# A two-layer decoder trunk on one core: attention scores two tiles apart, output projection by two blocks, weights of the tokens ahead of the first gather, expert output combined two weight tiles later

## The chip, the cores and the metric

The kernel runs on one core of one Trainium2 chip. The metric is device time in microseconds of one launch; three executions of the kernel before give its median. A separate profiled execution gives the trace. In it a busy TensorE is called PE, its weight loads PEld, VectorE DVE, ScalarE ACT, SyncE (which issues the weight loads) SP. Every time below is counted from the start of the profiled span.

## The reference

There are 256 tokens of width 1024 and two layers. Each layer adds a mixer of three branches and a feed-forward part; the second layer's feed-forward part has eight experts, of which each token uses two.

```python
for l in range(2):
    h = rms_norm(x, norm_mix[l]);  p = h @ w_in[l]          # split into xa, ba, ca, q, k, v, xc, gc, gates
    y_a = (ba * conv3(ca * xa)) @ wo_a[l]
    y_b = attention(q, k, v) @ wo_b[l]                       # 8 heads of 64, q and k normed and rotated, causal
    y_c = (gelu(gc) * rg_lru(conv4(xc))) @ wo_c[l]
    x = x + (sig(gA) * y_a + sig(gB) * y_b + sig(gC) * y_c) @ w_o[l]
    h = rms_norm(x, norm_ffn[l])
    x = x + (swiglu(h) if l == 0 else moe_swiglu(h))

def moe_swiglu(t, router, w_gate, w_up, w_down):             # 8 experts of width 3584
    top_v, top_i = top_k(t @ router, 2)
    comb = sum(one_hot(top_i, 8) * softmax(top_v)[..., None], axis=1)
    for e in range(8):
        out = out + comb[:, e, None] * (silu(t @ w_gate[e]) * (t @ w_up[e])) @ w_down[e]
```

## The kernel before

All weights are float32 and are read once, in loads of 1 MiB that SP issues. A load holds two weight tiles of 1024 columns. Each tile is split into a high part `whi`, an ACT copy (L175), and a low part `wlo`, a DVE subtraction (L176), and PE multiplies three times: high by high, high by low, low by high. Activations are split in the same way (`xn`, `xg`, `mo`, `x_e`, `y`; L194 on ACT and L195 on DVE). A tile is 24 matmuls of 256 columns in the dense stages (L184, L185, L187) and 6 of 512 columns in the expert stage (L972 gate and up, L1018 down).

`Flow` sets the order. `step` splits the tile that is two ahead, then issues the matmuls of the current tile, then runs what was put off with `flow.soon` (it runs after the matmuls of the next tile), and then takes entries from a queue, `rate` of them for each tile. `flow.push` appends to that queue. `flow.flush(n)` runs n of its entries at once. Where PE (or PE, DVE and ACT) is under a manual schedule, the instructions stand as they are issued; elsewhere a scheduler may move them.

**Scores.** `mixer` pushes the scores of head pairs 0 and 1 one after the other. A pair is eight small matmuls into two PSUM banks of the kind "at" (L596 and L598); DVE reads them with mask and maximum (L605), ACT takes exponentials (L609, which loads its table first) and scales them (L613).

**Output projection.** `mix_out` multiplies the merged branches `mo` by `w_o`. Before, a weight tile holds one block of 128 outputs over all eight k tiles, so the first tile already wants all eight parts of `mo`. In layer 0 two blocks share a bank and one addition of 128x512 takes both (`ev_o`); in layer 1 each block has its own (`ev_1`). After each pair of blocks `after` runs the next norm's part: `Moe.pair` in layer 1, with the router's sums `ps_l`, the squares `ps_v` and the transposed tokens `ps_tr`.

**Route.** `Moe.route` takes the root of the squares' sums on ACT (`rt`), selects two experts for each token on DVE (`sel`), counts places with two matmuls (`ps_r`) and builds a selection matrix `oh`. `start` gathers the tokens of the first two experts in eight groups (32 matmuls `ps_x`, split by L194 and L195 into `x_e`), and only then come the gate tiles; `weigh` (reciprocals, softmax of two, a count `ps_n`) and `slots` (`ps_rs`) are taken from the queue among them.

**Experts.** `rest` runs eight experts by seven chunks; a chunk is four gate tiles, four up tiles and four down tiles, the down tiles of a chunk beside the next chunk. In an expert's last chunk `ps_y` is complete after the second down tile for its first half and after the fourth for the second half. `split_act` then makes `y` from it, and `combine` (`ps_cb`, four matmuls, L1039, and two additions to `acc`, L1042) is put off with one `flow.soon`, so it stands after the next tile.

Of the kernel before, what the change touches and what calls it, by code (L numbers as in the profile page):

```python
# [17 lines left out]
P = 128  # L18
D = 1024
KT = 8  # L20
# [44 lines left out]
def trunk(ctx, tc, xt, cst, par, rgw, w_in, w_br, w_o, f_gu, f_d, m_g, m_u, m_d, out):  # L65
# [294 lines left out]
    def mixer(l, norm, br, mp):  # L360
# [324 lines left out]
        flow.push(hs[0][0], hs[1][0])  # L685
# [20 lines left out]
    def mix_out(l, ms, after, end=True):  # L706
        for hf in range(2):
            def ev_o(j, ps, hf=hf):
                q = 4 * hf + 2 * j
                dve.tensor_tensor(x2(q), x2(q), ps, OP.add)  # L710
                after(q // 2)

# [5 lines left out]
            blocks(w_o[l, hf], KT, ms, ev_o if end else ev_1, single=not end)  # L718
# [54 lines left out]
    class Moe:  # L773
# [9 lines left out]
        def pair(self, j):  # L783

            if j == 0:

                self.x = self.tile([P, 2, 3, KT, P], "x_e", FR)
                self.acc = self.tile([P, 2, D], "acc")
                self.h2h, self.h2l = two([P, 2, D], "h2")
                self.ps_l = [bank("sm", 3, "ps_l") for _ in range(2)]  # L790
                self.ps_v = [bank(t, b, "ps_v") for t, b in (("sm", 3), ("at", 2))]
# [10 lines left out]
            act.activation(sq, x2(2 * j), AF.Square)  # L802

# [6 lines left out]

            def squares():
                for t in range(2):
                    for k in (2 * j, 2 * j + 1):
                        pe.matmul(self.ps_v[t][:, 0:1], sq[:, k % 2, t * P:t * P + P], ones[:, 0:1], start=k == 0, stop=k == KT - 1)
# [16 lines left out]
            flow.soon(sums, squares, turn)  # L831
# [5 lines left out]

        def route(self):
            T = self.tile
            lg, self.rt = self.lg, T([P, 2], "rt")  # L840
            for t in range(2):
                act.activation(self.rt[:, t:t + 1], self.ps_v[t][:, 0:1], AF.Sqrt, bias=eps_t, scale=1.0 / D)
# [3 lines left out]
            sq, sel = small.tile([P, 2, S], F32, tag="sq", bufs=2, name="gt"), T([P, 2, 8], "sel", FR)  # L846
            gt, eq = (sq[:, i, 0:128].rearrange("p (t a b) -> p t a b", t=2, a=8) for i in range(2))
# [16 lines left out]
            self.sel = sel.bitcast(F32)  # L864

        def weigh(self):
# [4 lines left out]
            ps_n, cmax = bank("sm", 2, "ps_n"), T([P, 1], "cmax")  # L871
            pe.matmul(ps_n[:, 0:8], ones, sel[:, 0], start=True, stop=False)
            pe.matmul(ps_n[:, 0:8], ones, sel[:, 1], start=False, stop=True)
# [244 lines left out]
    with tc.tile_pool(name="psB", bufs=1, space=PSUM) as ps:  # L1118
        psums.append(ps)
        start()  # L1120
        with tc.manual_schedule(engines={PE, DVE, ACT}):
            rest()
# [100 lines left out]
```

## Time and profile before

| what | value |
|---|---|
| median of three runs | 1670.65 us (1670.14, 1670.65, 1673.53) |
| profiled execution | 1673.91 us |
| its span, first to last instruction | 1672.4 us |
| mean granted clock of PE | 0.993 |
| busy: PE, DVE, ACT | 98%, 81%, 70% |
| MB moved by DMA, mean rate | 472.03 MB, 282 GB/s |

A granted clock of 1.00 is 2.4 GHz and 0.50 is 1.2 GHz. The share of busy time is a mean over stages with different limits, and the expert stage, from about 678 us to the end, is over half of the span. In a timeline row the columns are start, duration, engine, line, operation and tiles, and in brackets how long the engine sat idle before it and for whom; matmuls overlap, so the pace of a row of matmuls is read from their starts. A row with "x4" holds four instructions that follow each other.

### The profile page before, as it was taken

The page shows a single profiled execution, that of the slowest core. Times are in us where ns is not written, and L with a number is a line of the kernel's source. Part 1 is how long each engine was busy: PE and PEld are TensorE (multiplying, and loading weights), DVE is VectorE, ACT ScalarE, POOL GpSimd, SP SyncE. Part 2 cuts the span into 40 slices and gives each one's busy share as a digit, 9 for nine tenths or more (in the row PEclk, how much of TensorE's full clock was granted, in tenths as well). Part 3 has the DMA queues.
Part 4 walks back from the last instruction along what each step waited for, and adds up shares of the span by engine and source line. Part 5 has one row for each costly group of instructions (what it writes and reads, how often), then busy time and mean ns, then how long its engine had stood idle before and what let it go on. Part 6 is the DMA issues. An engine that isn't in the chain of part 4 may idle for free.

```text
span 1672.4 us, 25362 instructions
## 1 busy us (share of the span) xinstructions
PE 1637.2 (98%) x9786; PEld 1439.9 (86%) x9786; DVE 1358.3 (81%) x1582; ACT 1178.4 (70%) x1443; POOL 0.7 (0%) x9
## 2 busy tenths in 40 slices
PE   6999999999999999999999999999999999999998
PEld 6989999999998999788888888888888888888886
DVE  7667777555676775889998999998999998999987
ACT  6577556444557755787777787777778777778775
POOL 0000000000000000000000000000000000000000
PEclk9999999999999999999999999999999999999999
DMA  8544555546653457799999999999999999999980
GB/s 322 184 150 152 198 181 182 197 142 222 227 178 128 158 199 308 298 370 364 354 362 346 353 365 376 343 367 332 352 365 368 353 362 339 339 377 370 347 335 27
DMA packets 67232, 472.03 MB, mean 282 GB/s; under 512 B 7456, under 2 KB 7584, under 8 KB 11040
## 3 DMA queue, kind: packets, MB, share of 16 engines
q1 hardware_dynamic: 66960, 470.19, 76.1%
q8 instruction: 78, 1.28, 0.3%
q14 instruction: 50, 0.41, 0.1%
q10 hardware_dynamic: 144, 0.16, 0.0%
HBM read 469.27 MB, written 1.05 MB: 281 GB/s over the span
## 4 chain that ended last, share of the span: by engine, by line
PE 91%; DVE 6%; issue 1%; ACT 1%; DMA 0%; SPq 0%; DVEq 0%; ACTq 0%
PE ps_gu L972 35%; PE ps_y L1018 16%; PE ps_mm L184 9%; PE ps_mm L187 9%; PE ps_mm L185 9%; DVE wlo L176 3%; PE ps_qk L478 3%; PE ps_tt L995 1%; PE ps_v L478 1%; PE ps_d L185 1%; PE ps_d L184 1%; PE ps_d L187 1%; PE ps_x L914 1%; DVE y L195 1%; DVE acc L1042 1%
## 5 line engine op out<-in xcount | busy, mean ns | idle before, releaser
L176 DVE TENSOR_TENSOR wlo<-raw,whi 128x1024 fp32r<-128x1024 f32 (+1 forms) x796 | 945.8, 1218 | 171.3 <-ACT whi L175 153.0
L175 ACT CAST whi<-raw 128x1024 fp32r<-128x1024 f32 (+1 forms) x796 | 824.1, 1051 | 328.8 <-PE ps_mm L185 138.9
L972 PE MATMUL ps_gu<-whi,x_e 128*128 128x512 f32 x1792 | 487.4, 394 | 0.0
L972 PEld LDWEIGHTS ps_gu<-whi,x_e 128*128 128x128 f32 x1792 | 330.8, 188 | 66.1
L972 PE MATMUL ps_gu<-wlo,x_e 128*128 128x512 f32 x896 | 276.4, 390 | 0.0
L1018 PE MATMUL ps_y<-whi,t 128*128 128x512 f32 x896 | 240.3, 390 | 0.0
L184 PE MATMUL ps_mm<-xn,whi 128*128 128x256 f32 x864 | 207.6, 282 | 0.0
L185 PE MATMUL ps_mm<-xn,whi 128*128 128x256 f32 x864 | 204.3, 279 | 0.0
L972 PEld LDWEIGHTS ps_gu<-wlo,x_e 128*128 128x128 f32 x896 | 168.2, 188 | 36.5
L1018 PEld LDWEIGHTS ps_y<-whi,t 128*128 128x128 f32 x896 | 167.3, 188 | 34.4
L184 PEld LDWEIGHTS ps_mm<-xn,whi 128*128 128x128 f32 x864 | 164.1, 190 | 3.8 <-issue 1.7
L185 PEld LDWEIGHTS ps_mm<-xn,whi 128*128 128x128 f32 x864 | 164.2, 190 | 0.1
L1018 PE MATMUL ps_y<-wlo,t 128*128 128x512 f32 x448 | 138.0, 389 | 0.0
L176 DVE TENSOR_TENSOR wlo<-more,whi 128x1024 fp32r<-128x1024 f32 x96 | 114.8, 1221 | 6.2 <-ACT whi L175 2.3
L187 PE MATMUL ps_mm<-xn,wlo 128*128 128x256 f32 x864 | 116.6, 278 | 0.0
L175 ACT CAST whi<-more 128x1024 fp32r<-128x1024 f32 x96 | 100.0, 1053 | 21.2 <-PE ps_gu L972 10.4
L187 PEld LDWEIGHTS ps_mm<-xn,wlo 128*128 128x128 f32 x864 | 107.1, 189 | 0.0
L1018 PEld LDWEIGHTS ps_y<-wlo,t 128*128 128x128 f32 x448 | 84.1, 188 | 17.7
L192 DVE TENSOR_TENSOR t<-ps_tt,t 128x512 fp32r<-128x512 f32 x56 | 38.8, 693 | 38.8 <-ACT t L191 38.8
L978 ACT ACTIVATE s<-ps_gu,rs 128x512 f32<-128x512 f32 x56 | 38.6, 689 | 43.3 <-PE ps_gu L972 43.3
L184 PE MATMUL ps_mm<-xg,whi 128*128 128x256 f32 x192 | 47.4, 287 | 12.6 <-ACT whi L175 12.6
L184 PEld LDWEIGHTS ps_mm<-xg,whi 128*128 128x128 f32 x192 | 37.2, 194 | 12.8 <-ACT whi L175 12.6
(242 smaller groups left out, 1637.4 us busy)
## 6 DMA issues: line engine op xcount, KB each, us to landing
raw<-in_m_g SPq DMA_DIRECT2D x98, 1024.0 KB, 6.8
raw<-in_m_u SPq DMA_DIRECT2D x96, 1024.0 KB, 7.0
raw<-in_m_d SPq DMA_DIRECT2D x94, 1024.0 KB, 6.7
raw<-in_w_in SPq DMA_DIRECT2D x54, 1024.0 KB, 4.8
raw<-in_f_gu SPq DMA_DIRECT2D x22, 1024.0 KB, 4.8
more<-in_m_u SPq DMA_DIRECT2D x16, 1024.0 KB, 6.8
more<-in_m_d SPq DMA_DIRECT2D x16, 1024.0 KB, 6.9
more<-in_m_g SPq DMA_DIRECT2D x14, 1024.0 KB, 6.8
```

The costliest lines, as they stand in the source:

```text
L175: act.copy(hi[:, :n], r)
L176: dve.tensor_tensor(lo[:, :n], r, hi[:, :n].bitcast(F32), OP.subtract)
L184: pe.matmul(ps, w, xh[k], start=first and k == 0, stop=False)
L185: pe.matmul(ps, w, xl[k], start=False, stop=False)
L187: pe.matmul(ps, wl[:, (at + k) * P:(at + k + 1) * P], xh[k], start=False, stop=last and k == n - 1)
L192: dve.tensor_tensor(lo, src, hi.bitcast(F32), OP.subtract)
L195: dve.scalar_tensor_tensor(lo, src, scale, hi.bitcast(F32), OP.mult, OP.subtract)
L478: pe.matmul(st["ps"][t], x[:, k, ts], w[:, o:o + 512], start=k == 0 and w is hi and x is hh, stop=k == KT - 1 and w is lo)
L914: pe.matmul(hold[f], src[:, t, f * P:f * P + P], oh[:, t].rearrange("p e s -> p (e s)"), start=i + t == 0, stop=i + t == 2)
L972: pe.matmul(ps, x[:, i_, k], w[:, o:o + 512], start=k == 0 and w is hi and i_ == 0, stop=k == KT - 1 and w is lo)
L978: act.activation(s, ps, AF.Silu, scale=rs)
L1018: pe.matmul(y, t[:, i, k * P:k * P + P], w[:, b * 512:b * 512 + 512], start=a and w is hi and i + b == 0, stop=z and w is lo and b == 1)
```

## The change

1. In both layers' `mixer` two empty queue entries stand between the scores of pair 0 and pair 1.
2. `mix_out` takes a weight tile as two blocks of 128 outputs over four k tiles; two tiles make two blocks, each in its own bank. The host lays `w_o` out for that. In the first pair's second tile the order of the halves is changed (`early`) so that k tiles 6 and 7 come last for both blocks. Every block is added to `x` by itself (128x256), in layer 0 too. In layer 1 PE's order from here to the end of `route` is now written out by hand.
3. In layer 1 the squares of pairs 0 to 2 are first added up on DVE, so `ps_v` takes 16 matmuls in place of 32. Two groups of eight matmuls of 256 columns (`idle`) that nobody reads are added in `route`. The low half of the last tokens stands before `oh`. `weigh` no longer holds the count and runs right behind the first group of the gather; four of the eight groups stand before the first gate tile, the other entries come two for each tile; `count` comes last.
4. `combine` is put off twice, and `y` has two buffers of its own.

```diff
-        flow.push(hs[0][0], hs[1][0])
+        flow.push(hs[0][0], *[lambda: None] * 2, hs[1][0])
...
-            blocks(w_o[l, hf], KT, ms, ev_o if end else ev_1, single=not end)
+            get, st = tiles(w_o[l, hf], KT * 512), {}
+            def mm(i, hf=hf, st=st, ev_1=ev_1):
+                def f(w):
+                    hi, lo = w
+                    xh, xl = ms()
+                    h = i % 2
+                    if h == 0:
+                        st["ps"] = [bank("mm", 3, "ps_mm")[:, 0:S] for _ in range(2)]
+                    early = h == 1 and i == 1 and hf == 0
+                    for b, half in ((0, 0), (1, 0), (0, 1), (1, 1)) if early else ((0, 0), (0, 1), (1, 0), (1, 1)):
+                        ps = st["ps"][b]
+                        for ks in [[(4 * b + n, 4 * h + n) for n in (2 * half, 2 * half + 1)]]:
+                            for o, k in ks:
+                                c = slice(o * P, o * P + P)
+                                pe.matmul(ps, hi[:, c], xh[:, k], start=k == 0, stop=False)
+                                pe.matmul(ps, hi[:, c], xl[:, k], start=False, stop=False)
+                            for o, k in ks:
+                                pe.matmul(ps, lo[:, o * P:o * P + P], xh[:, k], start=False, stop=k == KT - 1)
+                        if h == 1 and half == 1:
+                            ev_1(i - 1 + b, ps)
...
             act.activation(sq, x2(2 * j), AF.Square)
+            if j == 0:
+                self.sq = sq
+            elif j < 3:
+                dve.tensor_tensor(self.sq, self.sq, sq, OP.add)
+            else:
+                self.sq3 = sq
...
+        def squares(self, sq, first):
+            for t in range(2):
+                for i in range(2):
+                    pe.matmul(self.ps_v[t][:, 0:1], sq[:, i, t * P:t * P + P], ones[:, 0:1], start=first and i == 0,
+                              stop=not first and i == 1)
+        def idle(self, n):
+            ps = bank("mm", 3, "ps_w")
+            for _ in range(n):
+                pe.matmul(ps[:, :S], self.exact[:, 0], self.exact.rearrange("p t s -> p (t s)"), start=True, stop=True)
         def route(self):
+            self.squares(self.sq3, False)
+            self.idle(8)
...
+            self.idle(8)
+            self.low()
             self.oh0 = self.places(0, self.rk)
-            self.low()
...
-                            ys = pool.tile([P, 2, 512], FR, tag=tag, name="y")
+                            ys = self.tile([P, 2, 512], "y", FR, 2)
                             split_act(ys[:, 0], ys[:, 1], y, st["rs", e // 2][:, e % 2, 1:2])
                             fs = [combine(e, ys, q, t) for t in range(2)]
-                            if end and q == 0:
-                                fs = [lambda fs=fs: flow.soon(*fs)]
-                            flow.soon(*fs)
+                            flow.soon(lambda: flow.soon(*fs))
...
                     begin(0, self.oh0, "gu", 4)()
-                    flow.flush(KT + 1)
-                    flow.queue.extendleft((lambda: None, self.weigh))
+                    fs = [flow.queue.popleft() for _ in range(KT + 1)]
+                    fs[0]()
+                    self.weigh()
+                    for f in fs[1:4]:
+                        f()
+                    flow.queue.extendleft(reversed(fs[4:]))
+                    flow.push(self.count)
+                    flow.rate = 2.0
```

At the scores of layer 0 ACT's order changes. `sm` are the scores, `mx` their maximum and sum, `xcp` and `xcv` belong to branch C. Before:

```order
L613 ACTIVATE sm<-sm,mx 128x256
L609 ACTIVATE sm,mx<-sm,mx 128x128
L609 ACTIVATE sm,mx<-sm,mx 128x256
L609 ACTIVATE sm,mx<-sm,mx 128x128
L613 ACTIVATE sm<-sm,mx 128x128
L613 ACTIVATE sm<-sm,mx 128x256
L609 ACTIVATE sm,mx<-sm,mx 128x256
L175 CAST whi<-raw 128x1024
L613 ACTIVATE sm<-sm,mx 128x128
L613 ACTIVATE sm<-sm,mx 128x256
```

Now:

```order
L613 ACTIVATE sm<-sm,mx 128x256
L175 CAST whi<-raw 128x1024
L384 COPY xcp<-ps_mm 128x2x256
L175 CAST whi<-raw 128x1024
L390 ACTIVATE xcv<-xcp,par_t 128x256 x2
L609 ACTIVATE sm,mx<-sm,mx 128x128
L609 ACTIVATE sm,mx<-sm,mx 128x256
L175 CAST whi<-raw 128x1024
L613 ACTIVATE sm<-sm,mx 128x128
L613 ACTIVATE sm<-sm,mx 128x256
```

Two `whi` copies that stood behind the exponentials of pair 1 now stand ahead of them, right behind those of pair 0.

At the start of layer 0's output projection the order on DVE changes; `mg` are the merged branches, `mo<-mg,mo` makes the low part of two k tiles of `mo`, the first row here that of k tiles 4 and 5. Before:

```order
L176 TENSOR_TENSOR wlo<-raw,whi 128x1024
L195 SCALAR_TENSOR_TENSOR mo<-mg,mo 128x512
L661 TENSOR_TENSOR mg<-mg,gt 128x512
L195 SCALAR_TENSOR_TENSOR mo<-mg,mo 128x512
L176 TENSOR_TENSOR wlo<-raw,whi 128x1024
L710 TENSOR_TENSOR x_75<-x_75,ps_mm 128x512
L176 TENSOR_TENSOR wlo<-raw,whi 128x1024 x2
```

Now:

```order
L176 TENSOR_TENSOR wlo<-raw,whi 128x1024
L195 SCALAR_TENSOR_TENSOR mo<-mg,mo 128x512
L661 TENSOR_TENSOR mg<-mg,gt 128x512
L176 TENSOR_TENSOR wlo<-raw,whi 128x1024
L195 SCALAR_TENSOR_TENSOR mo<-mg,mo 128x512
L711 TENSOR_TENSOR x_75<-x_75,ps_mm 128x256 x2
L176 TENSOR_TENSOR wlo<-raw,whi 128x1024
```

One `wlo` now stands ahead of the last low part of `mo` (and one `whi` ahead of its high part on ACT).

At the end of expert 0 PE's order changes; the first row is the down tile that completes the first half of `ps_y`. Before:

```order
L1018 MATMUL ps_y<-wlo,t 128x512 x2
L1018 MATMUL ps_y<-whi,t 128x512 x4
L1018 MATMUL ps_y<-wlo,t 128x512 x2
L1039 MATMUL ps_cb<-y,ct 128x512 x4
L1018 MATMUL ps_y<-whi,t 128x512 x4
L1018 MATMUL ps_y<-wlo,t 128x512 x2
L972 MATMUL ps_gu<-whi,x_e 128x512 x4
L972 MATMUL ps_gu<-wlo,x_e 128x512 x2
L1039 MATMUL ps_cb<-y,ct 128x512 x4
```

Now:

```order
L1067 MATMUL ps_y<-wlo,t 128x512 x2
L1067 MATMUL ps_y<-whi,t 128x512 x4
L1067 MATMUL ps_y<-wlo,t 128x512 x2
L1067 MATMUL ps_y<-whi,t 128x512 x4
L1067 MATMUL ps_y<-wlo,t 128x512 x2
L1084 MATMUL ps_cb<-y,ct 128x512 x4
L1019 MATMUL ps_gu<-whi,x_e 128x512 x4
L1019 MATMUL ps_gu<-wlo,x_e 128x512 x2
L1019 MATMUL ps_gu<-whi,x_e 128x512 x4
L1019 MATMUL ps_gu<-wlo,x_e 128x512 x2
L1084 MATMUL ps_cb<-y,ct 128x512 x4
```

Each `ps_cb` group stands one weight tile later than it did.

## Rows read from the trace of the kernel before

**Rows 1.** The page, part 1: busy time, share of the span, instructions.
```profile
PE 1637.2 (98%) x9786; PEld 1439.9 (86%) x9786; DVE 1358.3 (81%) x1582; ACT 1178.4 (70%) x1443; POOL 0.7 (0%) x9
```

**Rows 2.** Timeline of PE at layer 0's scores, and an undisturbed pair later.
```profile
89.13 0.49 PE L596 MATMUL ps_s<-qk,qk 64*128 64x128 f32 x4
...
91.81 0.48 PE L596 MATMUL ps_s<-qk,qk 64*128 64x128 f32 x2 [1.76 <-DVE mx L605]
...
94.02 0.58 PE L184 MATMUL ps_mm<-xn,whi 128*128 128x256 f32 x1
...
97.84 0.28 PE L184 MATMUL ps_mm<-xn,whi 128*128 128x256 f32 x1
...
118.87 0.49 PE L596 MATMUL ps_s<-qk,qk 64*128 64x128 f32 x4
...
119.73 0.39 PE L184 MATMUL ps_mm<-xn,whi 128*128 128x256 f32 x1
```

**Rows 3.** Stretches: length, busy PE, PEld, DVE, ACT, POOL (count), granted clock, DMA share, GB/s.
```profile
92.70:96.10 3.40, 3.40 (x15) 2.75 (x16) 3.26 (x17) 3.39 (x12) 0.00 (x0) 0.50 0.01 2
...
505.70:512.60 6.90, 6.77 (x30) 6.12 (x31) 5.18 (x24) 6.89 (x24) 0.00 (x0) 0.51 0.01 4
...
669.50:676.50 7.00, 4.75 (x22) 4.69 (x23) 3.29 (x10) 3.58 (x8) 0.00 (x0) 0.51 0.84 355
...
730.36:747.19 16.83, 16.83 (x78) 13.92 (x77) 15.65 (x15) 13.51 (x15) 0.00 (x0) 1.00 1.01 377
```

**Rows 4.** Timeline of ACT behind layer 0's scores.
```profile
95.28 1.48 ACT L613 ACTIVATE sm<-sm,mx 128x128 f32<-128x128 f32 x4
...
99.11 1.03 ACT L175 CAST whi<-raw 128x1024 fp32r<-128x1024 f32 x1
```

**Rows 5.** Timeline of PE at layer 1's scores.
```profile
502.39 0.49 PE L596 MATMUL ps_s<-qk,qk 64*128 64x128 f32 x4
...
512.64 0.28 PE L184 MATMUL ps_mm<-xn,whi 128*128 128x256 f32 x1
```

**Rows 6.** Timeline of PE at the start of layer 0's output projection.
```profile
225.03 0.39 PE L185 MATMUL ps_mm<-mo,whi 128*128 128x256 f32 x1 [0.25 <-DVE mo L195]
...
226.30 0.50 PE L184 MATMUL ps_mm<-mo,whi 128*128 128x256 f32 x2 [0.29 <-ACT mo L194]
227.02 0.39 PE L185 MATMUL ps_mm<-mo,whi 128*128 128x256 f32 x1 [0.23 <-DVE mo L195]
```

**Rows 7.** Timeline of PE from layer 1's last output block into the experts.
```profile
666.14 0.51 PE L807 MATMUL ps_l<-gr,x 128*128 128x8 f32 x4
...
667.47 1.05 PE L814 MATMUL ps_v<-ones,sq 128*128 128x1 f32 x8
...
670.66 0.38 PE L858 MATMUL ps_r<-sel,exact 128*128 128x16 f32 x1 [1.57 <-DVE sel L855]
...
672.34 5.85 PE L914 MATMUL ps_x<-oh,h 128*128 128x256 f32 x32 [1.08 <-DVE oh L898]
678.03 1.09 PE L972 MATMUL ps_gu<-whi,x_e 128*128 128x512 f32 x4
...
685.01 1.07 PE L972 MATMUL ps_gu<-whi,x_e 128*128 128x512 f32 x4
```

**Rows 8.** Timeline of DVE there: the reciprocal that stands ahead of `sel`.
```profile
670.37 0.17 DVE L870 RECIPROCAL rt<-rt 128x2 f32<-128x2 f32 x1 [0.83 <-ACT warm L843]
```

**Rows 9.** Timeline of PE at the end of expert 0.
```profile
807.04 0.39 PE L1039 MATMUL ps_cb<-y,ct 128*128 128x512 f32 x1
807.66 0.96 PE L1039 MATMUL ps_cb<-y,ct 128*128 128x512 f32 x3 [0.23 <-DVE y L195]
808.46 1.08 PE L1018 MATMUL ps_y<-whi,t 128*128 128x512 f32 x4
```

**Rows 10.** Groups by line and shape, whole span: busy us, mean ns | idle before, releasers.
```profile
L176 DVE TENSOR_TENSOR wlo<-raw,whi 128x1024 fp32r<-128x1024 f32 x788 | 938.2, 1221 | 171.3 <-ACT whi L175 153.0 <-PE ps_gu L972 3.2 <-PE ps_y L1018 2.2
L175 ACT CAST whi<-raw 128x1024 fp32r<-128x1024 f32 x788 | 817.4, 1053 | 319.0 <-PE ps_mm L185 137.3 <-PE ps_gu L972 59.6 <-PE ps_y L1018 50.1
```

More of the change, by code (lines that the diff above doesn't have):

```diff
@@ L717, in ev_1 @@
                     after(k // 2)
-            blocks(w_o[l, hf], KT, ms, ev_o if end else ev_1, single=not end)
+            get, st = tiles(w_o[l, hf], KT * 512), {}
[18 more added lines that the diff above has]
+                            ev_1(i - 1 + b, ps)
+                return f
+            for i in range(4):
+                flow.step(lambda i=i, get=get: get(i), mm(i))
         if end:
@@ L788, in pair @@
                 self.acc = self.tile([P, 2, D], "acc")
+                self.tile([P, 2, 512], "y", FR, 2)
+                self.tile([P, 16], "lead")
                 self.h2h, self.h2l = two([P, 2, D], "h2")
                 self.ps_l = [bank("sm", 3, "ps_l") for _ in range(2)]
-                self.ps_v = [bank(t, b, "ps_v") for t, b in (("sm", 3), ("at", 2))]
+                self.ps_v = [bank("at", 2, "ps_v") for _ in range(2)]
                 self.exact = small.tile([P, 2, P], FR, tag="rstd", name="exact")
@@ L809, in sums @@
                     self.logits()
[L811 to L814, printed above, removed]
+                if j == 2:
+                    self.squares(self.sq, True)
             def turn():
@@ L843, in route @@
             act.activation(self.warm, self.rt[:, 0:1], AF.Silu)
-            sq, sel = small.tile([P, 2, S], F32, tag="sq", bufs=2, name="gt"), T([P, 2, 8], "sel", FR)
-            gt, eq = (sq[:, i, 0:128].rearrange("p (t a b) -> p t a b", t=2, a=8) for i in range(2))
+            ge, sel = T([P, 2, 128], "ge"), T([P, 2, 8], "sel", FR)
+            gt, eq = (ge[:, i].rearrange("p (t a b) -> p t a b", t=2, a=8) for i in range(2))
             la, lb = _b(lg, 2, [P, 2, 8, 8]), _b(lg, 3, [P, 2, 8, 8])
@@ L861, in route, with count @@
             dve.scalar_tensor_tensor(self.rk, ps_r[:, 0:16].rearrange("p (t e) -> p t e", t=2), 1.0, sel.bitcast(F32), OP.add, OP.mult)
+            self.idle(8)
+            self.low()
             self.oh0 = self.places(0, self.rk)
-            self.low()
             self.sel = sel.bitcast(F32)
+        def count(self):
+            T = self.tile
+            ps_n, cmax = bank("sm", 2, "ps_n"), T([P, 1], "cmax")
+            pe.matmul(ps_n[:, 0:8], ones, self.sel[:, 0], start=True, stop=False)
+            pe.matmul(ps_n[:, 0:8], ones, self.sel[:, 1], start=False, stop=True)
+            dve.tensor_reduce(cmax, ps_n[:, 0:8], AX.X, OP.max)
+            self.cint = T([P, 1], "cint", I32)
+            dve.tensor_copy(self.cint, cmax)
         def weigh(self):
@@ L1112, in trunk @@
         m = Moe(ep)
-        mix_out(1, ms, m.pair, False)
-        start, rest = m.experts(None, True)
-        flow.settle()
-        flow.flush()
-        m.route()
+        with tc.manual_schedule(engines={PE}):
+            mix_out(1, ms, m.pair, False)
+            start, rest = m.experts(None, True)
+            flow.settle()
+            flow.flush()
+            m.route()
     with tc.tile_pool(name="psB", bufs=1, space=PSUM) as ps:
         psums.append(ps)
-        start()
         with tc.manual_schedule(engines={PE, DVE, ACT}):
+            start()
             rest()
```

18 lines of the change are left out of this document (4 added, 14 removed).

## The prediction

> **What bounds the kernel now.** First the busy shares: PE works in 98% of the span [rows 1], so nothing can be won but what PE still loses to waits, to a lower clock, and to matmuls that are taken out. Next the granted clock by stretch, and the timelines of PE where it falls: the reader is to see that both come in a few places. Then the groups by line, for who waits for whom in the expert stage. A dense weight tile is 24 matmuls of 256 columns, an expert tile 6 of 512. In a steady chunk of the experts PE is never idle for 16.83 us [rows 3]; twelve tiles and four small transposes of about 0.13 us stand in it, so an expert tile takes about 1.36 us, one 512-column matmul 0.227 us, and a dense tile, with twice the columns, 2.72 us. These paces price everything below. The sum is made against the profiled execution, 1673.91 us; it lies 3.26 us above the median of the three runs, 1670.65.
>
> **Scores, both layers.** Pair 0 and pair 1 stand back to back from 89.13 to 94.02, 4.89 us; a pair that finds its banks free takes 0.86 us (118.87 to 119.73) [rows 2]. The second pair waits 1.76 us for DVE's read of the first pair's banks (L605, `mx`) [rows 2]. Right behind that wait the granted clock is 0.50, 1.2 GHz, for 3.4 us in layer 0, and 0.51 for 6.9 us in layer 1 [rows 3], so the tile that starts at 94.02 takes 3.82 us in place of 2.72 [rows 2]. The two empty entries let two tiles run between the pairs, and that is time enough for DVE. What is late next is ACT: the third tile wants its `whi`, and the new order of ACT has it right behind the scaling of pair 0. Nothing ahead of that scaling changes, so it still ends at about 96.7 (95.28 plus 1.48 us for four overlapping instructions), and a `whi` of 1.03 us ends at about 97.75 [rows 4]. PE's sequence from 89.13 is then: 0.86 (pair 0), 2.72, 2.72, 0.86 (pair 1) to 96.29, a new wait until 97.8, and the third tile to 100.52. Before, the first tile ends at 97.84 and two more at 2.72 end at 103.28, by which time the same work is done. Gain 2.76 us. Layer 1 runs the same rows 413.26 us later (502.39 against 89.13), but there the clock stays low longer and the first tile ends at 512.64 [rows 5], two more at 518.08; the new sequence ends at 100.52 + 413.26 = 513.78. Gain 4.30 us. The new wait, some 1.5 us in each layer, is all that this costs; were `whi` there in time, the gain would be 1.5 us more in each, and if the clock falls in the new wait, about 1.7 us less in each (half of the 3.4 us at half speed).
>
> **Output projection, layer 0.** Here the first tile wants all parts of `mo`, and PE waits 0.25, 0.29 and 0.23 us for them [rows 6]. A wait costs more than its bracket: the `ps_cb` group of rows 9 is idle for 0.23 us yet takes 1.42 us where four matmuls need 0.91, that is 0.28 us beyond. With some 0.17 us for each I take 1.27 us in all. After, k tiles 4 and 5 are wanted at 2.72 us from the start of the first tile and 6 and 7, by the `early` order, at 4.08 us. But DVE now has a `wlo` ahead of the last low part, and ACT a `whi` of 1.05 us ahead of its high part, which waits for PE to free a buffer at the end of the first tile (2.7 us). The high part lands at about 4.3 us, the low part at about 5.75 us. In order that would be a wait of 1.5 us; here a scheduler sets PE's order and has put other matmuls of the next blocks between, which leaves about 0.4 us. Gain 0.85 us, and about 0.15 us at the first tile of the feed-forward part, whose last part of the input comes in smaller pieces: 1.0 us, between -0.3 (the whole 1.5 us is waited) and 1.4. Four more additions on DVE lie under 11 us of matmuls in each half.
>
> **Output projection, layer 1.** Sixteen `ps_v` matmuls go; eight take 1.05 us [rows 7], 0.96 by the pace behind them, so 16 are 1.8 us. Against that PE's order is now by hand, and nothing stands between to cover the low part of `mo`: the 1.5 us above is waited in full, where the scheduler had covered it. About half a microsecond of small waits on PSUM banks and `x` goes with the old order (an estimate; the bound from below is none). Net gain 0.75 us, between 0 and 2.4.
>
> **Route.** From the end of the last output block (666.14) to the fifth gate tile (685.01) PE takes 18.87 us, with waits of 1.57 us for `sel` and 1.08 us for `oh` [rows 7]. The last `ps_l` and `ps_v`, then `sel`, are a chain: `sel` stands on DVE behind a reciprocal that waits 0.83 us for ACT's table load [rows 8]. Moving that reciprocal into `weigh` frees `sel` by about 0.5 us, since the low half of `h` now fills part of the gap; `oh` stands behind it and comes 0.5 us earlier too. The gather is 32 matmuls from 672.34 to 678.03, 5.7 us [rows 7], mostly at a clock of 0.51 [rows 3]; half of it now stands among the gate tiles. `weigh` is a chain of about a dozen small DVE steps of 0.17 us with one ACT step, some 2.5 us, which now stands on DVE ahead of the low parts `x_e`; the gate tile waits for it, where before it lay under gate tiles. Following the new order by hand, the gather starts 5.7 us after the last block, the first gate tile at 8.8, the fifth at 17.3. Gain 1.55 us. The two groups of idle matmuls lie in PE's waits: eight at 0.113 us are 0.9 us at full clock, 1.7 at half, against waits of 1.57 and 1.08 us. If the clock holds there it speeds up the gather, but the gate tile then waits for `weigh` anyway. Bounds: 0 (the idle matmuls outlast the second wait by 0.7 us and `weigh` takes a microsecond more) to 3.
>
> **Combine.** `y`'s low part is queued on DVE behind two `wlo` of 1.22 us each [rows 10]; the `ps_cb` group waits for it and takes 1.42 us in place of 0.91 [rows 9]. There are fourteen such groups in experts 0 to 6, two for each, of 1.38 to 1.46 us; the last expert's stand at the end and stay. One tile later, 1.36 us, `y` has long landed (the wait was 0.23 us), and the accumulator's additions come later on a DVE that is busy 15.65 of 16.83 us in a chunk [rows 3], in an order that still has each `wlo` some 0.4 us ahead of PE. Gain 14 x 0.5 = 7.0 us. A second buffer for `y` costs no instruction.
>
> The loads could take this back. In the steady chunk the DMA engines' share is 1.01 and they move 377 GB/s [rows 3], so there is little above that. Yet ACT's idle time ahead of `whi` is put down to PE first, 319.0 us with no DMA among its three largest releasers [rows 10]: the loads run ahead, and a chunk itself gets no shorter, only the seams between experts do. The Trainium skill (DMA: Bandwidth & Descriptors, Specifications) puts what one core can draw from HBM at about 358 GB/s, by which the stage would stay as long as it is or give back part of the 7 us. The steady chunk's 377 GB/s speaks against that rule as a cap on this core.
>
> **Sum.** 2.76 + 4.30 + 1.0 + 0.75 + 1.55 + 7.0 = 17.4 us, so 1673.91 - 17.4 = 1656.5 us for an execution like the profiled one. The median execution is 3.26 us faster than that; some of this is probably the very clock that the change wins back (the stretch at 0.51 is twice as long in layer 1 as in layer 0 and need not be so in each execution), so I subtract half of it: **1655 us**.
>
> **The rivals.**
> - The clock falls again in the new ACT waits of the scores (1.5 us). For: a wait of 1.76 us brought it down [rows 2, 3], and one of 1.57 us stands where it fell in the route [rows 7, 3]. Against: the new wait is shorter than either. Price 1.7 us a layer: 1658.5. Chance 0.17.
> - The combine's wait moves instead of going: `y` or the additions run late because DVE has only 1.18 us to spare in a chunk [rows 3], and PE then waits for `wlo`. Half to all of 7.0 us is lost: 1658.5 to 1662. Chance 0.10.
> - The loads set the pace of the expert stage, as weighed above. Then ACT would wait for DMA, and the 7.0 us reappear there: 1662. Chance 0.05, since PE and not a DMA is what ACT waits for now [rows 10].
> - The change doesn't do what it says: layer 1's hand order and the route give back what they win, waits on banks included (up to 3 us), and the scores and the combine win half. 17.4 shrinks to about 3: 1668. Chance 0.04.
> - Slower: `wlo` becomes the bound of the expert stage. The new `y` and the moved tiles change where buffers lie; if DVE's subtraction gets slower thereby, each chunk's spare 1.18 us is used up once a `wlo` takes 0.1 us more, 1.32 us. At 1.36 us the 56 chunks of 12 cost 56 x 12 x 0.04 = 27 us: 1682. Against: 788 of them lie at many addresses and average 1221 ns [rows 10]. Chance 0.04.
>
> **How the numbers follow.** The forecast's own case has 0.60, from 1651 (the bounds of the scores' `whi` and of the route go well) to 1659. The range leaves out the last two rivals and the outer ends: 1650.5 to 1662. A measurement of this kernel tells 0.2%, 3.3 us, from no change; faster by more than that holds all cases but the last two, 0.91; within it 0.05; slower 0.04.
>
> **What would show it.** Right: pair 1's scores in a slot of 0.86 us, ACT's `whi` as the releaser of the next tile with about 1.5 us, no stretch at 0.50 behind the scores; fourteen `ps_cb` groups of 0.91 us with no wait on `y`; the fifth gate tile about 17.3 us after the last output block; layer 1's projection some 28.3 us long with a wait on `mo` of about 1.5. Wrong: a wait on `wlo` or on a DMA in the expert stage, chunks longer than 16.83 us, the clock still at half behind the scores, or a first gate tile that waits for `x_e` far beyond 8.8 us.

## The result

The changed kernel takes 1651.58 us (median of four runs, 1650.85 to 1657.01) against 1671.59 us for the kernel before on the same occasion: a ratio of 0.9885 (95% interval 0.9864 to 0.9906). That lies in the forecast's range, 3.4 us below its 1655 us. Its profiled execution takes 1650.99 us, its span is 1648.9 us; the one before took 1673.91. That is 22.9 us, where the sum said 17.4. The place of the difference is read by laying the starts of PE's stages side by side.

| stretch of PE | forecast gain | before | after | gain |
|---|---|---|---|---|
| start to the first scores (not touched) | 0 | 89.13 | 87.04 | 2.09 |
| layer 0, first scores to output projection | 2.76 | 133.19 | 128.61 | 4.58 |
| output projection of layer 0 to the end of the feed-forward part | 1.0 | 205.33 | 204.21 | 1.12 |
| layer 1, first scores to output projection | 4.30 | 134.73 | 128.72 | 6.01 |
| output projection of layer 1 to its last matmul | 0.75 | 28.90 | 28.22 | 0.68 |
| last output matmul to the fifth gate tile | 1.55 | 18.99 | 17.40 | 1.59 |
| fifth gate tile to PE's end | 7.0 | 980.00 | 972.43 | 7.57 |

The gains add up to 23.6 us. The two stretches that the table leaves out, from layer 1's start to its first scores (74.75 and 74.78 us) and behind PE's end (7.38 and 7.52), give 0.2 back, which leaves the 23.5 us by which the spans differ.

The page of the changed kernel: busy time, GB/s in the 40 equal slices of the span, and the chain of work that ended last. Below it stands the same chain line of the kernel before:

```profile
PE 1624.7 (99%) x9786; PEld 1434.7 (87%) x9786; DVE 1359.1 (82%) x1588; ACT 1178.6 (71%) x1443; POOL 0.7 (0%) x9
...
GB/s 334 187 170 141 200 191 185 201 145 217 218 179 166 142 208 339 312 353 377 362 365 341 355 363 379 352 369 337 348 369 379 355 369 335 351 367 377 356 330 28
...
PE 97%; DVE 1%; ACT 1%; DMA 0%; issue 0%; SPq 0%; DVEq 0%; ACTq 0%
```

```profile
PE 91%; DVE 6%; issue 1%; ACT 1%; DMA 0%; SPq 0%; DVEq 0%; ACTq 0%
```

The number of PE's instructions is the same as in [rows 1]; the sixteen idle matmuls stand in the place of the sixteen of `ps_v`. The chain that ended last ran 91% through PE before and 97% now.

At layer 0's scores, PE and then ACT (timelines):

```profile
87.04 0.49 PE L596 MATMUL ps_s<-qk,qk 64*128 64x128 f32 x4
...
93.55 0.49 PE L596 MATMUL ps_s<-qk,qk 64*128 64x128 f32 x4
93.87 0.60 PE L598 MATMUL ps_s<-qk,qk 64*128 64x256 f32 x4
94.40 0.39 PE L184 MATMUL ps_mm<-xn,whi 128*128 128x256 f32 x1
...
97.24 0.28 PE L184 MATMUL ps_mm<-xn,whi 128*128 128x256 f32 x1
```

```profile
92.86 1.49 ACT L613 ACTIVATE sm<-sm,mx 128x128 f32<-128x128 f32 x4
94.25 1.04 ACT L175 CAST whi<-raw 128x1024 fp32r<-128x1024 f32 x1
```

Against [rows 2]: both pairs take 0.85 us, and the third tile starts at 94.40, right behind pair 1 and 0.9 us before the `whi` that the prediction thought it needs is ready (94.25 plus 1.04). That copy is the fourth tile's, which starts at 97.24. The granted clock over both mixers' scores (length, busy PE, PEld, DVE, ACT, POOL, clock, DMA share, GB/s), and where it is still low:

```profile
86.00:104.00 18.00, 18.00 (x158) 17.08 (x158) 16.00 (x45) 17.47 (x39) 0.00 (x0) 1.00 0.47 152
494.00:512.00 18.00, 18.00 (x159) 17.08 (x158) 15.98 (x45) 17.36 (x39) 0.00 (x0) 1.00 0.46 154
654.90:658.40 3.50, 3.40 (x17) 3.07 (x16) 2.40 (x12) 1.91 (x5) 0.00 (x0) 0.51 1.02 426
```

Of the three low stretches of [rows 3], those of the scores are gone, and the route's is half as long. At the end of expert 0 and in the route (timeline of PE):

```profile
792.53 1.07 PE L1084 MATMUL ps_cb<-y,ct 128*128 128x512 f32 x4
793.44 1.07 PE L1019 MATMUL ps_gu<-whi,x_e 128*128 128x512 f32 x4
...
796.16 1.07 PE L1084 MATMUL ps_cb<-y,ct 128*128 128x512 f32 x4
797.07 1.07 PE L1019 MATMUL ps_gu<-whi,x_e 128*128 128x512 f32 x4
```

```profile
651.69 0.28 PE L838 MATMUL ps_l<-gr,x 128*128 128x8 f32 x2
...
655.69 0.35 PE L900 MATMUL ps_r<-sel,exact 128*128 128x16 f32 x1
655.90 0.35 PE L901 MATMUL ps_r<-sel,exact 128*128 128x8 f32 x1
656.11 2.05 PE L876 MATMUL ps_w<-exact 128*128 128x256 f32 x8
658.27 2.16 PE L961 MATMUL ps_x<-oh,h 128*128 128x256 f32 x16
660.27 1.08 PE L1019 MATMUL ps_gu<-whi,x_e 128*128 128x512 f32 x4
...
668.97 1.17 PE L1019 MATMUL ps_gu<-whi,x_e 128*128 128x512 f32 x4
```

`ps_cb` takes 0.91 us, and so do all fourteen groups; in [rows 9] the first took 1.42. The fifth gate tile starts 17.28 us after the first `ps_l`, where [rows 7] have 18.87.

### The profile page after: what moved, and what is told of

Its sections match the earlier page's. It is cut to its first block, busy times and chain, and to the rows that moved or that the text cites. A ratio compares the mean times of both kernels' runs of the same rounds, so it can differ in the third digit from the quotient of the medians.

```text
span 1648.9 us, 25382 instructions
## 1 busy us (share of the span) xinstructions
PE 1624.7 (99%) x9786; PEld 1434.7 (87%) x9786; DVE 1359.1 (82%) x1588; ACT 1178.6 (71%) x1443; POOL 0.7 (0%) x9
## 4 chain that ended last, share of the span: by engine, by line
PE 97%; DVE 1%; ACT 1%; DMA 0%; issue 0%; SPq 0%; DVEq 0%; ACTq 0%
PE ps_gu L1019 37%; PE ps_y L1067 19%; PE ps_mm L184 9%; PE ps_mm L187 9%; PE ps_mm L185 9%; PE ps_qk L478 3%; PE ps_tt L1044 1%; PE ps_v L478 1%; PE ps_d L185 1%; PE ps_d L184 1%; PE ps_d L187 1%; PE ps_x L961 1%; PE ps_mm L732 1%; PE ps_mm L731 1%; PE ps_mm L734 1%; PE ps_cb L1084 1%
## 5 line engine op out<-in xcount | busy, mean ns | idle before, releaser
L184 PE MATMUL ps_mm<-xn,whi 128*128 128x256 f32 x864 | 204.8, 280 | 0.0
L185 PE MATMUL ps_mm<-xn,whi 128*128 128x256 f32 x864 | 202.0, 277 | 0.0
L184 PEld LDWEIGHTS ps_mm<-xn,whi 128*128 128x128 f32 x864 | 162.3, 188 | 3.1 <-issue 2.3
L185 PEld LDWEIGHTS ps_mm<-xn,whi 128*128 128x128 f32 x864 | 162.3, 188 | 0.1
L184 PE MATMUL ps_mm<-xg,whi 128*128 128x256 f32 x192 | 47.4, 287 | 10.1 <-ACT whi L175 10.0
L185 PE MATMUL ps_mm<-xg,whi 128*128 128x256 f32 x192 | 46.6, 283 | 1.3 <-DVE xg L195 1.3
```

Of the source, the lines that this page charges most:

```text
L184: pe.matmul(ps, w, xh[k], start=first and k == 0, stop=False)
L185: pe.matmul(ps, w, xl[k], start=False, stop=False)
```

## The experiments

**Scores alone, in the kernel before.**

```diff
-        flow.push(hs[0][0], hs[1][0])
+        flow.push(hs[0][0], *[lambda: None] * 2, hs[1][0])
```

> The kernel before with the two empty entries between the scores of pairs 0 and 1 alone. The prediction's step (the third tile waits 1.5 us for its whi): the span loses 2.76 + 4.30 = 7.1 us against the kernel before, and ACT's whi is the releaser of a wait behind pair 1's scores in each layer. Rival, read from the trace of the changed kernel (whi of the third tile stands ahead of the exponentials of pair 0 already, the split being two tiles ahead): no wait there, 4.6 us in layer 0 and 6.0 in layer 1, 10.6 in all, and no stretch at a granted clock of 0.50 behind the scores.

1661.82 us, ratio to the kernel before 0.9953 (0.9936 to 0.9969). From the first scores to the output projection it takes 128.72 us in each layer: 4.47 and 6.01 us less, 10.5 in all, and no wait for `whi`. The rival holds: the whole gain of the scores comes from the two entries, and the step with ACT's new wait was wrong.

**PE kept busy in the wait, in the kernel before.** The scores of pair 1 get sixteen matmuls ahead of them that nobody reads:

```diff
-        flow.push(hs[0][0], hs[1][0])
+        def filled():
+            xh, _ = norm.parts()
+            ps = bank("mm", 3, "ps_w")
+            for _ in range(16):
+                pe.matmul(ps[:, :S], xh[:, 0][:, :P], xh[:, 0], start=True, stop=True)
+            hs[1][0]()
+        flow.push(hs[0][0], filled)
```

> The kernel before with 16 matmuls of 128x256 whose result nobody reads between the scores of pair 0 and pair 1, so that PE works through the 1.76 us of its wait for DVE. If the clock falls because PE stands idle in that wait, it stays at 1.00 behind the scores, the two slots stay near 4.9 us or get shorter by what the low clock cost inside them, and the tile behind each takes 2.72 us: about 1.1 us less in layer 0 and 2.5 to 3.3 in layer 1, 3.6 to 5 in all. If the small score matmuls themselves bring it down, it falls as before and nothing is won.

1667.33 us, ratio 0.9979 (0.9969 to 0.9989), with work added. Timeline of PE, and the stretch behind the scores of layer 1:

```profile
88.52 2.17 PE L689 MATMUL ps_w<-xn 128*128 128x256 f32 x16
90.62 0.85 PE L596 MATMUL ps_s<-qk,qk 64*128 64x128 f32 x3
...
91.95 0.38 PE L184 MATMUL ps_mm<-xn,whi 128*128 128x256 f32 x1
...
94.77 0.28 PE L184 MATMUL ps_mm<-xn,whi 128*128 128x256 f32 x1
```

```profile
500.60:508.60 8.00, 8.00 (x66) 7.36 (x65) 7.00 (x31) 7.94 (x25) 0.00 (x0) 1.00 0.24 102
```

The clock stays at 1.00, the slot shrinks from 4.89 to 4.28 us and the tile behind it to 2.82 (91.95 to 94.77). The two mixers take 131.58 and 131.59 us: 1.6 and 3.1 us less, 4.7 of the 10.6. So what the idle PE costs by its clock is nearly as much as what it costs by the wait itself (2.9 us in each layer, 131.58 against the 128.72 of the run before). The runs agree: the ten of this kernel have a mean granted clock of 0.996 or 0.997, the thirteen of the kernel before beside them 0.993 to 0.997 with 0.994 in the middle. The fall doesn't follow every such wait: in the profile of the kernel with the combination alone (below), PE waits 1.38 and 0.26 us in layer 0 and the clock stays at 1.00; its mixer takes 131.09 us. In the profile of the buffers alone, 1.39 and 0.26 us at the same place are followed by 3.4 us at a clock of 0.50.

**One entry in place of two, in the changed kernel** (`*[lambda: None] * 1`).

> The changed kernel with one empty entry in place of two: pair 1 stands one weight tile behind pair 0. In the trace of before DVE has read pair 0's banks 3.3 us after the pair's first matmul; one tile later is 0.86 + 2.72 = 3.58 us. By that the second entry buys nothing: pair 1's slots of 0.86 us, the same time as the changed kernel within 0.3 us from the first scores to the end of each mixer. Rival: DVE's or ACT's other work gets between, the slot grows by 0.3 to 1 us and the clock may fall again.

1654.01 us, ratio 0.9902 (0.9885 to 0.9918). The pair's slot is 0.86 us, as the theory has it, but the mixers take 129.76 and 130.24 us, 1.15 and 1.5 more than with two entries. PE's waits from 60 to 680 us (total, times, longest), and ACT's timeline:

```profile
PE ps_mm L184 <- ACT whi L175: 1.1, 2, 0.7
```

```profile
97.84 0.79 ACT L613 ACTIVATE sm<-sm,mx 128x128 f32<-128x128 f32 x2
98.54 0.49 ACT L609 ACTIVATE sm<-sm,mx 128x256 f32<-128x256 f32 x1
...
99.03 1.03 ACT L175 CAST whi<-raw 128x1024 fp32r<-128x1024 f32 x1
```

The `whi` stands behind the exponentials of both pairs again, as in [rows 4], and PE waits for it, 0.36 us in layer 0 and 0.72 in layer 1. Here is the wait that the prediction put into the changed kernel, at the fourth tile and shorter; the clock stays at 1.00 behind it. The two waits are 1.1 of the 2.7 us that this kernel loses in the mixers. The rest builds up in the tiles behind them, where the rows show no wait. One entry is enough for DVE; the second is what lets ACT copy two weight tiles between the pairs.

**Combination alone, and buffers alone, in the kernel before.** The first has the change's order of the combination, with `y` in its two buffers, which are set aside at the start of the expert stage together with a small unused tile (`lead`):

```diff
+                self.tile([P, 2, 512], "y", FR, 2)
+                self.tile([P, 16], "lead")
...
-                            pool, tag = (raws, "raw") if end and q else (state, "x0")
-                            ys = pool.tile([P, 2, 512], FR, tag=tag, name="y")
+                            ys = self.tile([P, 2, 512], "y", FR, 2)
                             split_act(ys[:, 0], ys[:, 1], y, st["rs", e // 2][:, e % 2, 1:2])
                             fs = [combine(e, ys, q, t) for t in range(2)]
-                            if end and q == 0:
-                                fs = [lambda fs=fs: flow.soon(*fs)]
-                            flow.soon(*fs)
+                            flow.soon(lambda: flow.soon(*fs))
```

> The kernel before with the combination two weight tiles later and y in its own two buffers, and nothing else of the change. The prediction: fourteen ps_cb groups of 0.91 us in place of 1.42, 7.0 to 7.1 us less between the fifth gate tile and the end of PE, no wait on y in experts 0 to 6. Rival: part of the 7.6 us that the changed kernel wins there comes from the gather's half among the gate tiles; then 0.4 to 0.5 us are missing here beside the 7.1. Rival that the wait moves to wlo: under 4 us.

1662.55 us, ratio 0.9954 (0.9937 to 0.9971). The groups take 0.91 us; from the fifth gate tile to the end of PE 972.34 us against 980.00, 7.66 less. This is the whole of the 7.57 that the changed kernel wins there; none of it comes from the gather.

The second keeps the single `flow.soon` and the case of the last expert, and changes only where `y` lies:

```diff
+                self.tile([P, 2, 512], "y", FR, 2)
+                self.tile([P, 16], "lead")
...
-                            pool, tag = (raws, "raw") if end and q else (state, "x0")
-                            ys = pool.tile([P, 2, 512], FR, tag=tag, name="y")
+                            ys = self.tile([P, 2, 512], "y", FR, 2)
```

> The kernel before with y in two buffers of its own, but combined after one weight tile as before. Theory: the wait is for DVE's queue, not for a buffer: fourteen ps_cb groups of 1.38 to 1.46 us as before, 0 us. Rival: the single buffer held the split back; groups of 0.91 to 1.1 us and 4 to 7 us less.

1671.28 us, ratio 0.9998 (0.9988 to 1.0009): nothing. Its timeline of PE reads as [rows 9]:

```profile
803.98 0.39 PE L1041 MATMUL ps_cb<-y,ct 128*128 128x512 f32 x1
804.60 0.96 PE L1041 MATMUL ps_cb<-y,ct 128*128 128x512 f32 x3 [0.23 <-DVE y L195]
805.40 1.08 PE L1021 MATMUL ps_y<-whi,t 128*128 128x512 f32 x4
```

So DVE's queue was waited for, not a buffer, and the moved buffers didn't make `wlo` slower either: its mean is 1222 ns here, 1221 in [rows 10].

**Without the early order, in the changed kernel.**

```diff
-                    early = h == 1 and i == 1 and hf == 0
+                    early = False
```

> The changed kernel without the early order: the first pair's second tile takes block 0 over all its k tiles, then block 1, so block 0 wants mo's k tiles 6 and 7 half a block (0.68 us) sooner. Theory: what is late is the low part of mo on DVE, behind a wlo; layer 1's wait of 0.95 us grows by 0.68 to about 1.6 and its output projection from 28.2 to 28.9 us; layer 0's, which the scheduler orders, by 0 to 0.7 us. Rival: the order covers nothing, both stay within 0.2 us.

1656.52 us, ratio 0.9899 (0.9852 to 0.9947); two runs that lie 6.6 us apart, so the stage is read from the trace. Layer 1's projection takes 28.75 us against 28.22, and PE waits for the high part of `mo` too:

```profile
PE ps_mm L732 <- DVE mo L195: 0.9, 1, 0.9
PE ps_mm L731 <- ACT mo L194: 0.8, 1, 0.8
```

0.53 us, near the 0.68 expected, but with ACT as the new releaser where the theory had DVE's wait grow. Layer 0's took 22.90 us against 22.26, which is not shown to be the order: the changed kernel itself took 22.89 in another profile (last section).

**Without the idle matmuls, in the changed kernel.** Both `self.idle(8)` are taken out.

> The changed kernel without the two groups of eight matmuls whose result nobody reads. The prediction's view (the gate tile waits for the weights' chain and x_e on DVE whatever the clock): from the last output block to the fifth gate tile 17.4 us within 0.5, the clock low for longer (up to 6.8 us as before). Rival: the clock stays low into the gate tiles and the same stretch takes 18.5 to 19.5 us. Third: the eight matmuls of the second group delay the gather (they end at 658.2, oh at 657.2) and leaving them out gains up to 1 us.

1651.71 us, ratio 0.9882 (0.9861 to 0.9902), and 18.69 us from the last output matmul to the fifth gate tile against 17.40. The gather starts sooner, but at half the clock (timeline of PE, and the low stretch):

```profile
657.13 3.75 PE L959 MATMUL ps_x<-oh,h 128*128 128x256 f32 x16 [1.09 <-DVE rk L1176]
660.68 1.74 PE L1017 MATMUL ps_gu<-whi,x_e 128*128 128x512 f32 x4
```

```profile
655.20:662.10 6.90, 5.56 (x22) 5.22 (x23) 4.88 (x21) 4.15 (x8) 0.00 (x0) 0.51 0.81 342
```

Sixteen `ps_x` take 3.55 us here and 2.0 with the idle matmuls; the first gate tile is slowed too. In this pair of profiles the rival holds: the route is not bound by the weights' chain alone, the clock decides. But one pair doesn't settle it, since the clock there differs between executions, and by their runs the two kernels can't be told apart (0.9882, and 0.9885 for the changed kernel).

**The changed kernel once more.**

> The changed kernel itself once more, for the granted clock in the route, which differs between executions of one program. Six profiled executions without the idle matmuls were low for 6.83 us there; five with them were low for 0, 3.41, 3.41, 6.83 and 6.83 us. Theory: the idle matmuls shorten the stretch in part of the executions; then 17.1 to 17.4 us from the last output block to the fifth gate tile where it is 3.41 or none, near 19.0 where it is 6.83.

1650.43 us. The clock does not fall in the route at all, and the stretch takes 17.13 us. Now the gather starts sooner than in the first profile, and the first gate tile waits for the tokens, whose low parts stand behind `weigh` on DVE (timeline of PE):

```profile
657.34 2.12 PE L961 MATMUL ps_x<-oh,h 128*128 128x256 f32 x16
660.04 1.19 PE L1019 MATMUL ps_gu<-whi,x_e 128*128 128x512 f32 x4 [0.57 <-DVE x_e L195]
```

Over all profiles the low stretch lasted 6.8 us in each of the six without idle matmuls (18.69 us in the one that has the rest of the change). With them it was none, none, 3.4 and 3.4 us in the four that have the rest of the change in the route unaltered and otherwise little touched (17.13, 17.13, 17.37, 17.40 us), and 6.8 us in the kernel without the early order (19.02 us). Where the clock falls for that long anyway, the idle matmuls cost 0.3 us (19.02 against 18.69); where it doesn't, they are worth 1.3 to 1.6. The five profiles with the old route, all at 6.8 us, take 18.69 to 19.38 us, so at that clock the changed route wins 0.7 us at most. What decides which it is stays open.

**The whole gather ahead of the first gate tile, in the changed kernel.** The tokens' weights (`weigh`) go back among the gate tiles with it:

```diff
-                    fs = [flow.queue.popleft() for _ in range(KT + 1)]
-                    fs[0]()
-                    self.weigh()
-                    for f in fs[1:4]:
-                        f()
-                    flow.queue.extendleft(reversed(fs[4:]))
-                    flow.push(self.count)
-                    flow.rate = 2.0
+                    flow.flush(KT + 1)
+                    flow.queue.extendleft((self.count, self.weigh))
```

> The changed kernel with the whole gather ahead of the first gate tile and the tokens' weights among the gate tiles again, the rest of the change kept. Theory: the gain of the route (1.6 us from the last output block to the fifth gate tile) is the moved reciprocal and squares, 0.5 us, plus the gather's half that overlaps; without the overlap the stretch takes 18 to 18.5 us against 17.4. Rival: the overlap buys nothing, since the gate tiles then wait for the weights' chain; 17.4 as before.

1651.14 us, ratio 0.9878 (0.9858 to 0.9899). The profile has 19.86 us to the fifth gate tile, with the clock low for 6.8 us and a wait of 0.67 us of `ps_rs` for the weights. By its runs it can't be told from the changed kernel. So the same kernel once more:

> The kernel with the whole gather ahead of the first gate tile once more, since its first profile had the clock low for 6.83 us (19.86 us from the last output block to the fifth gate tile). If the clock is low for 3.41 us or not at all here, the gather's split alone is what is left against 17.4: theory 18 to 18.5 us. If it is low for 6.83 us again, 19.9, to be compared with the 19.0 of the split gather at the same clock: 0.8 us for the split.

1652.13 us; 18.37 us with the clock low for 3.4 us, against 17.40 of the changed kernel at the same. At 6.8 us it was 19.86 against 19.02. At either clock the split gather with the early `weigh` is worth 0.8 to 1.0 us (the two were not run apart), of which 0.67 is the wait for the weights:

```profile
PE ps_rs L975 <- DVE rc L939: 0.7, 1, 0.7
```

**A version that waits less.** Three edits to the changed kernel, each aimed at a wait in its list:

```profile
PE ps_tt L1044 <- DVE x_e L195: 2.6, 2, 1.3
PE ps_mm L185 <- DVE xg L195: 1.3, 2, 0.9
PE ps_mm L732 <- DVE mo L195: 1.0, 1, 1.0
```

```diff
                     if c == 3 and e % 2 == 1 and e + 1 < NE:
+                        flow.due = 0.8
                         flow.push(begin(e // 2 + 1))
...
-    def mm3(ps, wh, wl, at, xh, xl, first, last):
+    def mm3(ps, wh, wl, at, xh, xl, first, last, late=False):
...
-            pe.matmul(ps, w, xl[k], start=False, stop=False)
+            if not late:
+                pe.matmul(ps, w, xl[k], start=False, stop=False)
         for k in range(n):
-            pe.matmul(ps, wl[:, (at + k) * P:(at + k + 1) * P], xh[k], start=False, stop=last and k == n - 1)
+            pe.matmul(ps, wl[:, (at + k) * P:(at + k + 1) * P], xh[k], start=False, stop=last and not late and k == n - 1)
+        for k in range(n if late else 0):
+            pe.matmul(ps, wh[:, (at + k) * P:(at + k + 1) * P], xl[k], start=False, stop=last and k == n - 1)
...
                     for b, half in ((0, 0), (1, 0), (0, 1), (1, 1)) if early else ((0, 0), (0, 1), (1, 0), (1, 1)):
+                        if early and half == 1:
+                            ko = [(4 * b + n, 4 + n) for n in (2, 3)]
+                            for w in (hi, lo):
+                                for o, k in ko:
+                                    pe.matmul(st["ps"][b], w[:, o * P:o * P + P], xh[:, k], start=False, stop=False)
+                            if b == 1:
+                                for d in (0, 1):
+                                    for n in (2, 3):
+                                        o = 4 * d + n
+                                        pe.matmul(st["ps"][d], hi[:, o * P:o * P + P], xl[:, 4 + n], start=False, stop=n == 3)
+                                    ev_1(d, st["ps"][d])
+                            continue
```

`late` is set for the first tile of the feed-forward part and of the second mixer.

> The changed kernel with three further edits aimed at what PE still waits for in its trace. (1) The gathers of the later expert pairs start from the same phase of the queue each time, so that no gather group stands right ahead of the transposes ps_tt: two waits of 1.29 us for x_e go, about 2.8 us. (2) In the output projection's early tile the two products that want the low part of mo's last k tiles come last: the wait of 0.95 us in layer 1 and that of about half as much in layer 0 shrink to near 0, 1 to 1.3 us. (3) In the first tile of the feed-forward part and of the second mixer the products with the low part of x come last: waits of 0.87 and 0.42 us, 1 us. Theory: 4.5 to 5 us less than the changed kernel on the span from the first scores. Rival: the ACT parts of the same inputs are only half a microsecond earlier and the wait moves to them; then (2) and (3) give less than 1 us together and the whole is 3 to 3.5.

1647.77 us, ratio 0.9863 (0.9841 to 0.9885): the lowest median of all, with an interval that overlaps the changed kernel's, so the gain is read from the trace. From the first scores to PE's end it takes 1551.20 us, 3.17 less than the changed kernel's 1554.37 (another profile of that: 1554.55). The gathers' phase gives 1.83 us of it (of 2.6 us of waits), layer 1's projection 0.81, the two first tiles 0.50 together, layer 0's projection nothing. For `xg` the rival holds; the wait went to the engine that makes the other half:

```profile
PE ps_mm L184 <- ACT xg L197: 1.1, 2, 0.9
```

## Why the prediction was right, and where it was not

**Scores: right mechanism, one step wrong, 3.5 us too small.** Both the wait for DVE and the low clock behind it go, as said, and `fill` shows that the clock's share (4.7 of 10.6 us) is caused by PE standing idle, in these executions. In the two other profiles with the old scores the clock fell for a shorter time or not at all in one layer, and against them the gain would be 8.6 and 8.4 us. The step "the third tile wants its `whi`, and the new order of ACT has it right behind the scaling of pair 0" was wrong by one tile: weights are split two tiles ahead, and that copy is the fourth tile's. The text had the price of being wrong there, 1.5 us in each layer, and 2.76 + 1.5 and 4.30 + 1.5 lie 0.3 and 0.2 us below the 4.58 and 6.01 measured. The error is one of reading an order as if each copy served the tile next to it; counting the copies from the start of the stage to the tile would have shown it. `one_entry` shows that wait where it does exist.

**Output projections: right for layer 0, right by luck in part for layer 1.** Layer 0 wins 1.38 us to the feed-forward part and gives 0.26 back there, where the first tile's wait for `xg` grew from 0.60 to 0.87 us. The text had 0.85 and another 0.15 at that tile: no wait on `mo` is left where it kept 0.4, and the second was of the wrong sign. Layer 1's net of 0.68 is the 0.75 forecast, but by two misses that cancel. Its wait for `mo` is 0.95 by the bracket, not the 1.5 forecast, and so the rest wins 1.6, not the 2.3 of 16 `ps_v` and the small waits; of those one even grew (`ps_l` waits 0.39 us for `x`, 0.17 before). Neither projection's layout nor the sixteen `ps_v` that went were run alone.

**Route: the sum right by luck.** The gather was to start at 5.7 us after the last block, the first gate tile at 8.8, the fifth at 17.3; the trace, counted in the same way from the first router matmul at 651.69, has 6.6, 8.6 and 17.3. The text drew its 1.55 us from the moved reciprocal and the gather's half and put the clock at nothing: "If the clock holds there it speeds up the gather, but the gate tile then waits for `weigh` anyway". That holds between 3.4 us of low clock and none, 17.40 and 17.13 us: where the clock holds, the gate tile waits 0.57 us. It does not hold at 6.8 us, where the stretch takes 18.7 to 19.0 us, no less than 18.69, the shortest of the old route. So most of the 1.59 us measured, if not all, is the shorter low stretch. The idle matmuls do outlast PE's wait, as feared: `oh` is there 5.5 us after the first router matmul, the gather starts at 6.6.

**Combine: right.** Fourteen groups of 0.91 us without a wait on `y`; 7.57 us where 7.0 was forecast, with 14 x 0.51 = 7.1 from the groups and the rest, some 0.03 us each, in the tile beside them. The rivals of the combine fall with it: no wait on `wlo`, and the additions stay ahead. So does that of the loads: the stage became shorter by all that the groups won, and the slices of the page reach 379 GB/s in it. That is above the limit of about 358 GB/s that the Trainium skill gives for one core (DMA: Bandwidth & Descriptors, Specifications); the trace disagrees with that figure as a cap on this core.

**The clock rival** did not come true: the new waits that it hung on do not exist. **The rest of the 22.9 us** is not the change. PE's first matmul starts at 12.60 us in the profile before and at 10.02 after, waiting for ACT's first `whi`; over all profiles, whose code is the same there, it lies between 9.9 and 12.8 us. The profiled execution of before lay 3.26 us above its median, which the text put down in part to the clock. The late start may be 2.6 of it; that isn't shown, since runs without a profile show no start. The clock does have a part in such differences: of the later runs of that kernel, nineteen with a granted clock of 0.993 or 0.994 average 1672.2 us and ten with 0.995 to 0.997 average 1670.1.

**Small slips in the sums.** At the pace of 0.96 us for eight, 16 `ps_v` are 1.9 us and not 1.8; layer 1's terms as written give 0.8 and not 0.75; a gain of 3 us in place of 17.4 gives 1669 us by the same steps and not 1668. None of them bears on the forecast.

## What to carry to other kernels

Two bursts of work that share a PSUM bank pair can be spaced. Here that cost nothing and saved twice, the wait and, where it fell, the clock behind it. But count what each of the other engines does between them, since one tile of space was enough for DVE and two were needed for ACT. A reader of an in-order pipeline that works ahead has to count from the start which tile a preparation belongs to, and not take the nearest. When a consumer waits for the end of another engine's queue, moving it one step later can be worth more than a buffer: the buffers alone gave nothing here, the step with them 7.6 us. The step without them was not run. And where a forecast comes out right, check each of its terms: two of these six came out by errors that cancel, or by a clock that the text had put at nothing.

## What the runs showed of the hardware

The projection of layer 0 runs at one of two paces at the same granted clock. In the changed kernel's first profile and in its second, the same 13 us hold 117 and 113 matmuls, PE busy throughout (length, busy PE, PEld, DVE, ACT, POOL, clock, DMA share, GB/s):

```profile
223.00:236.00 13.00, 13.00 (x117) 13.00 (x117) 11.18 (x18) 9.63 (x15) 0.00 (x0) 1.00 0.60 212
```

```profile
223.00:236.00 13.00, 13.00 (x113) 13.00 (x112) 11.00 (x17) 9.11 (x15) 0.00 (x0) 1.00 0.59 207
```

A 256-column matmul follows the other at 0.117 us in place of 0.113, and the projection takes 22.89 us in place of 22.26. It came and went between executions of one program, in either layer; nothing in the rows explains it. The layout's gain in layer 0 is there at the slow pace too: the old layout takes 24.36 us in its one profile at that pace (combination alone) and 23.64 or 23.65 in the others.

The clock's fall behind an idle PE is not sure either. In the three profiles with the old scores PE waits twice at this place in each layer, the second time for 0.26 us. In layer 0 the clock fell for 3.4 us behind a first wait of 1.76 us and behind one of 1.39, and not at all behind one of 1.38. In layer 1 the first wait is 1.76 or 1.77 us each time, and the clock fell for 3.4 us in one profile and 6.8 us in two.
